# Sums of squares of keys and queries as ScalarE's accumulated output, one token block at a time

## The chip, the core and the metric

The kernel runs on one core of a Trainium2 chip. The core's engines are TensorE (PE; PEld is its weight load), VectorE (DVE), ScalarE (ACT), GpSimd (POOL) and SyncE (SP), which run side by side and wait for each other by semaphores; 16 DMA engines move data. Matmuls write into PSUM, everything else lies in SBUF. The metric is the device time of one execution, in microseconds.

## The reference

Two layers of a diffusion block on 256 context and 256 latent tokens of width 1024. Each layer has a mixer, whose heads read one modulated input, and an MLP of 4096 hidden columns, each behind a residual and a layer norm. Half of the mixer's width are four heads of a gated delta rule of width 128. For those, keys, queries and values go through a convolution over the tokens and a silu; keys and queries are then divided by their norm and rotated (latent tokens only):

```python
def l2norm(x):
    return x * rsqrt(sum(square(x), axis=-1) + 1e-6)

qkv = silu(centred_conv(qkv, conv_w))          # 5 taps over the tokens
q, k, v = split(qkv)                            # (tokens, 4 heads, 128) each
q, k = l2norm(q), l2norm(k)
q, k = rope_2d(q, rope), rope_2d(k, rope)       # latent tokens
q = q * 128 ** -0.5
```

The change lies in the sum of squares of `l2norm`. In the second layer only latent tokens leave the block, so queries are wanted for latent tokens alone.

## The kernel before

The 512 tokens are four blocks of 128 (blocks 0 and 1 context, 2 and 3 latent). Projections are computed with channels on the partitions and tokens in the columns. A float32 product is made of three matmuls (`mm3`, L276 to L278) of operands split in a high and a low part; ScalarE makes the high part of a weight tile (L250), VectorE the low part (L252).

Each layer is a mixer and an MLP. A string in the configuration gives the order in which a mixer's parts are written down (H is a delta-rule head, B and C the gates' two halves, X the end of this stage), but the order in which an engine gets its instructions is laid out by the framework's scheduler, which simulates the engines with its own costs and takes what it thinks is ready. Each engine then runs its list strictly in order. So work of other parts (the projections' matmuls, weight splits, the gates, adaLN matmuls L303) stands between the steps of a head.

`gdn_head(h)` runs a head's key (kind 0), query (kind 1) and value. For key and query the chain of steps is:

- `gdn_conv`: ScalarE copies the projected channels out of PSUM (L530) and scales them by the middle tap (L531); VectorE adds the other four taps (L533); ScalarE takes a tanh (L535), VectorE makes the silu (L536); TensorE transposes four blocks, so that tokens are on the partitions (L540, into PSUM tile `gtr`).
- ScalarE copies `gtr` to SBUF (L550: `ktok` for a key, a rotating buffer shown as `XT` for a query), squares it (L552); VectorE sums each block over its 128 columns (L554) into the four columns of `gss` and adds the epsilon (L555); POOL raises this to the power -0.5 (L231, inside `rsq`), which gives `grs`.
- The rotation of the latent blocks: POOL makes the sine part in two instructions (L561), VectorE the cosine part (L562) and their sum (L563).
- A key is multiplied by `grs` (L565); a query keeps `grs` apart, scaled (`rq`, L567). TensorE transposes the result back (L570, PSUM tile `gtb`), and ScalarE copies it out (L571).

POOL also adds the column mask to the attention bias (L681), 1.85 us in this stage. There are 4 heads x 2 kinds x 2 layers = 16 such places: 12 with four token blocks, 4 (queries of the second layer) with two.

Of the kernel before, what the change touches and what calls it, by code (L numbers as in the profile page):

```python
# [15 lines left out]
AF = mybir.ActivationFunctionType  # L16
ALU = mybir.AluOpType
AX = mybir.AxisListType
# [158 lines left out]
def body(ctx, tc, a, out, dump=None):  # L177
    nc = tc.nc
    V, S, G, PE, SP = nc.vector, nc.scalar, nc.gpsimd, nc.tensor, nc.sync
# [8 lines left out]
    def sm(name):  # L188
        return PP.tile([128, 512], F32, name=name, tag="g", bufs=CFG["g"])
# [37 lines left out]
    def small(shape, name, dt=F32, bufs=3):  # L227
        return P0.tile(shape, dt, name=name, tag="sm_" + name, bufs=bufs)

    def rsq(outp, x, m):  # L230
        G.tensor_tensor(outp, x, m, op=ALU.pow)  # L231
# [237 lines left out]
    def mixer(l, hT, pre, ctx_m):  # L469
# [22 lines left out]
        def ar(name):  # L492
            cnt[0] += 1
            i = cnt[0] % 8
            return XT[:, 4 * i:4 * i + 4].rearrange("p a b -> p (a b)")
# [20 lines left out]
        def gdn_conv(h, kind):  # L516
            b = 3 * h + kind
            lat_only = last and kind == 1
            t0 = 256 if lat_only else 0
            sg = 1 if lat_only else 0  # L520
            if b in pre:
                ps = pre[b]["ps"]
            else:
                ps = proj_T(getw("w_gdn", l, b), t0, "psg")
            psv = ps.rearrange("p (s c) -> p s c", s=2)
            cnt[1] += 1
            cin = cins[:, cnt[1] % CFG["cin"]]
            ac = ar("cacc")
            av = ac.rearrange("p (s c) -> p s c", s=2)[:, sg:]
            S.activation(cin[:, sg:, 2:258], psv[:, sg:], AF.Copy)  # L530
            S.activation(av, psv[:, sg:], AF.Copy, scale=cw[:, b, 2:3])  # L531
            for kk in (0, 1, 3, 4):
                V.scalar_tensor_tensor(av, cin[:, sg:, kk:kk + 256], cw[:, b, kk:kk + 1], av, op0=ALU.mult, op1=ALU.add)  # L533
            th = ar("cth")
            S.activation(th[:, t0:], ac[:, t0:], AF.Tanh, scale=0.5)  # L535
            V.scalar_tensor_tensor(ac[:, t0:], th[:, t0:], 1.0, ac[:, t0:], op0=ALU.add, op1=ALU.mult)  # L536
            q0 = 2 if lat_only else 0
            pt = sm("gtr").rearrange("p (t c) -> p t c", t=4)
            for t in range(q0, 4):
                PE.transpose(pt[:, t], ac[:, 128 * t:128 * t + 128], ident)  # L540
            return pt, q0
# [4 lines left out]
        def gdn_head(h):  # L546
            for kind in (0, 1):
                pt, q0 = gdn_conv(h, kind)
                x = ktok[h] if kind == 0 else ar("qtok").rearrange("p (t c) -> p t c", t=4)
                S.activation(x[:, q0:], pt[:, q0:], AF.Copy)  # L550
                sq = ar("gsq").rearrange("p (t c) -> p t c", t=4)
                S.activation(sq[:, q0:], pt[:, q0:], AF.Square)  # L552
                ss, rs = small([128, 4], "gss", bufs=4), small([128, 4], "grs", bufs=4)
                V.tensor_reduce(ss[:, q0:], sq[:, q0:], axis=AX.X, op=ALU.add)  # L554
                V.tensor_scalar(ss[:, q0:], ss[:, q0:], 4 * NORM_EPS, None, op0=ALU.add)  # L555
                rsq(rs[:, q0:], ss[:, q0:], mh[:, q0:4])
                x_ = x[:, 2:4]
                ra = ar("rope")[:, :256].rearrange("p (t c) -> p t c", t=2)
                hv = lambda ap, i: ap.rearrange("p t (a s c) -> p (t a) s c", a=2, s=2)[:, :, i]
                for i in range(2):  # L560
                    G.tensor_tensor(hv(ra, i), hv(x_, 1 - i), hv(sinT, i), op=ALU.mult)  # L561
                V.tensor_tensor(x_, x_, cosT, op=ALU.mult)  # L562
                V.tensor_tensor(x_, x_, ra, op=ALU.add)  # L563
                if kind == 0:
                    V.tensor_tensor(x, x, rs.unsqueeze(2).to_broadcast([128, 4, 128]), op=ALU.mult)  # L565
                else:
                    V.tensor_scalar(rq[:, q0:, h], rs[:, q0:], 128.0 ** -0.5, None, op0=ALU.mult)  # L567
                pb = sm("gtb").rearrange("p (t c) -> p t c", t=4)
                for t in range(q0, 4):
                    PE.transpose(pb[:, t], x[:, t], ident)  # L570
                S.activation(kqT[h][:, kind].rearrange("p (t c) -> p t c", t=4)[:, q0:], pb[:, q0:], AF.Copy)  # L571
            pt, _ = gdn_conv(h, 2)
            S.activation(vtok[h], pt, AF.Copy, scale=0.5)
# [197 lines left out]
        def run_order(o):  # L771
            for c in o:
                if c in "fBC":
                    {"f": fill, "B": gates1, "C": gates2}[c]()
                    continue
                i = cnt2[c]
                cnt2[c] += 1
                if c == "H":
                    gdn_head(i)
                elif c == "N":  # L780
                    proj_nv(i)
                elif c in "KQ":
                    proj_qk(i, "KQ".index(c))
                elif c == "Z":
                    proj_z(i)
                else:
                    tt = [t for t in CFG["tord"] if t in to]
                    attend(i // len(tt), tt[i % len(tt)], biases[i // len(tt)])
# [576 lines left out]
```

## Time and profile before

| | |
|---|---|
| three runs | 1256.89, 1257.86, 1259.34 us; median 1257.86 |
| profiled execution | 1260.03 us, its span 1258.2 us |
| mean granted TensorE clock | 0.989 |
| delta-rule heads of layer 0 / layer 1 | about 50 to 128 us / 790 to 862 us |

The profile is of one execution. Its page gives busy times by engine; the views used below are the busy time in stretches of the span (windows), the waits of one engine by what it waited for, groups of instructions of one shape, and the timeline. In a timeline row stand the start, the length, the engine, the line, the operation with output and inputs, how many instructions the row holds, and in brackets how long the engine had been idle and what ended that. Lengths overlap on a pipelined engine, so a matmul of 0.39 us may be followed by the next one after 0.23.

### The profile page before, as it was taken

Reading aid. Unit: us, or ns where it says so; the run is one execution under the profiler, and the core shown is the slowest. Engines: PE = TensorE matmul, PEld = TensorE weight load, DVE = VectorE, ACT = ScalarE, POOL = GpSimd, SP = SyncE. Lnnn points to the kernel's source line nnn. Section 1 sums busy time; section 2 is a strip of 40 time slices with the busy share of each in tenths; the row PEclk is TensorE's granted clock in tenths of the full one; section 3 lists DMA queues with packets and bytes.
Section 4 is the critical chain, followed back from the end, with each engine's and each line's share of the span. In section 5 each row is a group of like instructions: output and inputs, shape, how many; then the busy total and the mean of one; then the engine's idle time right before and its main releaser. Section 6 shows DMA issues by size and latency. Waiting matters only on the chain. (4 is left out here: it accounts for less than half of the span.)

```text
span 1258.2 us, 20332 instructions
## 1 busy us (share of the span) xinstructions
PE 1208.7 (96%) x7848; PEld 981.4 (78%) x7848; DVE 865.1 (69%) x1732; ACT 608.7 (48%) x1115; POOL 88.2 (7%) x98
## 2 busy tenths in 40 slices
PE   7999999999999999999999999899999998999997
PEld 3676568887878987787788888676679886898996
DVE  3798697666489954444444478996876768766677
ACT  2465637665446632322322356566466554544551
POOL 0132000100101000000000000222000110000000
PEclk9999999999999999999999999899999998999999
DMA  9623570225166633544533256225730457555552
GB/s 327 233 67 114 171 249 19 64 61 175 64 234 198 220 118 117 157 132 121 158 128 104 97 184 202 84 84 177 268 106 30 138 166 279 179 189 185 189 189 92
DMA packets 62721, 190.91 MB, mean 152 GB/s; under 512 B 7809, under 2 KB 17825, under 8 KB 62625
## 3 DMA queue, kind: packets, MB, share of 16 engines
q1 hardware_dynamic: 62624, 189.62, 45.9%
q8 instruction: 62, 1.02, 0.3%
q14 instruction: 35, 0.28, 0.1%
HBM read 187.46 MB, written 2.13 MB: 151 GB/s over the span
## 5 line engine op out<-in xcount | busy, mean ns | idle before, releaser
L252 DVE TENSOR_TENSOR wlo<-wraw,whi 128x1024 fp32r<-128x1024 f32 x224 | 275.5, 1232 | 185.7 <-ACT whi L250 185.2
L250 ACT ACTIVATE whi<-wraw 128x1024 fp32r<-128x1024 f32 x224 | 236.9, 1059 | 320.1 <-PE pst L278 169.6
L276 PE MATMUL pm<-hhi,whi 128*128 128x256 f32 (+1 forms) x544 | 176.3, 324 | 0.8 <-ACT whi L250 0.7
L278 PE MATMUL pm<-hhi,wlo 128*128 128x256 f32 (+1 forms) x544 | 174.5, 321 | 0.0
L277 PE MATMUL pm<-hlo,whi 128*128 128x256 f32 (+1 forms) x544 | 174.4, 321 | 0.0
L276 PE MATMUL pst<-whi,ah 128*128 128x512 f32 x384 | 150.0, 391 | 0.0
L277 PE MATMUL pst<-wlo,ah 128*128 128x512 f32 x384 | 149.5, 389 | 0.0
L278 PE MATMUL pst<-whi,al 128*128 128x512 f32 x384 | 149.1, 389 | 0.0
L276 PEld LDWEIGHTS pm<-hhi,whi 128*128 128x128 f32 x544 | 103.5, 190 | 14.4 <-issue 5.8
L278 PEld LDWEIGHTS pm<-hhi,wlo 128*128 128x128 f32 x544 | 103.6, 190 | 7.8
L277 PEld LDWEIGHTS pm<-hlo,whi 128*128 128x128 f32 x544 | 103.6, 190 | 7.2
L276 PEld LDWEIGHTS pst<-whi,ah 128*128 128x128 f32 x384 | 72.1, 188 | 15.5 <-issue 0.8
L278 PEld LDWEIGHTS pst<-whi,al 128*128 128x128 f32 x384 | 72.1, 188 | 15.2
L276 PE MATMUL psg<-hhi,whi 128*128 128x512 f32 (+1 forms) x216 | 79.5, 369 | 4.6 <-ACT XT L531 2.3
L277 PEld LDWEIGHTS pst<-wlo,ah 128*128 128x128 f32 x384 | 72.1, 188 | 14.4
L278 PE MATMUL psg<-hhi,wlo 128*128 128x512 f32 (+1 forms) x216 | 79.0, 366 | 0.6 <-DVE wlo L252 0.6
L277 PE MATMUL psg<-hlo,whi 128*128 128x512 f32 (+1 forms) x216 | 79.1, 367 | 0.0
L533 DVE SCALAR_TENSOR_TENSOR XT<-U,cw,XT 128x512 f32<-128x512 f32 (+1 forms) x96 | 65.5, 702 | 1.9 <-ACT XT L531 1.6
L1243 ACT ACTIVATE ah<-mr 128x256 fp32r<-128x256 f32 (+1 forms) x68 | 33.4, 491 | 65.7 <-DVE mr L1241 65.7
L303 PE MATMUL adaps<-wraw,scT 128*32 128x256 f32 x640 | 55.5, 389 | 3.2 <-DMA wraw<-w_ada 3.1
L231 POOL TENSOR_TENSOR rs<-ve,mh 128x1 f32<-128x1 f32 x12 | 12.2, 1018 | 630.4 <-DVE bmv L396 362.5
L1244 DVE TENSOR_TENSOR al<-mr,ah 128x256 fp32r<-128x256 f32 (+1 forms) x68 | 35.1, 516 | 24.3 <-ACT ah L1243 24.1
(672 smaller groups left out, 2387.2 us busy)
## 6 DMA issues: line engine op xcount, KB each, us to landing
wraw<-w SPq DMA_DIRECT2D x140, 512.0 KB
wraw<-w_ada SPq DMA_DIRECT2D x80, 512.0 KB
wraw<-w_gdn SPq DMA_DIRECT2D x27, 512.0 KB
wraw<-w_out SPq DMA_DIRECT2D x24, 512.0 KB
xa<-w_ada SPq DMA_DIRECT2D x32, 256.0 KB
wraw<-w_vz SPq DMA_DIRECT2D x16, 512.0 KB
wraw<-w_na SPq DMA_DIRECT2D x16, 512.0 KB
lnrow<-lnr SPq DMA_DIRECT2D x8, 512.0 KB
```

Of the source, the lines that this page charges most:

```text
L231: G.tensor_tensor(outp, x, m, op=ALU.pow)
L250: S.activation(hi, r, AF.Copy)
L252: V.tensor_tensor(lo, r, hi.bitcast(F32), op=ALU.subtract)
L276: PE.matmul(o, l[0], r[0], start=start, stop=False)
L277: PE.matmul(o, l[0], r[1], start=False, stop=False)
L278: last_mm[:] = [PE.matmul(o, l[1], r[0], start=False, stop=stop).ins]
L303: PE.matmul(st["ps"][32 * g:32 * g + 32, :256], scT[:, k, :], w[:, 256 * g:256 * g + 256], start=(k == 0), stop=(k == 7), tile_position=(0 ...
L533: V.scalar_tensor_tensor(av, cin[:, sg:, kk:kk + 256], cw[:, b, kk:kk + 1], av, op0=ALU.mult, op1=ALU.add)
L1243: S.activation(ah, r, AF.Copy)
L1244: V.tensor_tensor(al, r, ah.bitcast(F32), op=ALU.subtract)
```

## The change

The Square of the whole tile and the reduce on VectorE go. Instead, ScalarE squares each token block by itself, with an accumulated output that writes the sum over the block's 128 columns into one column of `gss`. So at a place with four blocks ScalarE runs four instructions of 128 columns instead of one of 512, and VectorE one instruction less. The buffers stay the same.

```diff
                 S.activation(x[:, q0:], pt[:, q0:], AF.Copy)
                 sq = ar("gsq").rearrange("p (t c) -> p t c", t=4)
-                S.activation(sq[:, q0:], pt[:, q0:], AF.Square)
                 ss, rs = small([128, 4], "gss", bufs=4), small([128, 4], "grs", bufs=4)
-                V.tensor_reduce(ss[:, q0:], sq[:, q0:], axis=AX.X, op=ALU.add)
+                for t in range(q0, 4):
+                    S.activation(sq[:, t], pt[:, t], AF.Square, accum_out=ss[:, t:t + 1])
                 V.tensor_scalar(ss[:, q0:], ss[:, q0:], 4 * NORM_EPS, None, op0=ALU.add)
                 rsq(rs[:, q0:], ss[:, q0:], mh[:, q0:4])
```

The framework lays the instructions out anew. POOL's order in the first head stays as it was; the other engines' lists differ in both mixers. Three places of layer 0 are shown.

VectorE at the first key head (`ktok_456`), in the list before, from the weight split L252 to the key's product with `grs`:

```order
L252 TENSOR_TENSOR wlo<-wraw,whi 128x1024
L554 TENSOR_REDUCE gss<-XT 128x4
L562 TENSOR_TENSOR ktok_456<-ktok_456,cst 128x256
L555 TENSOR_SCALAR gss<-gss 128x4
L536 SCALAR_TENSOR_TENSOR XT<-XT 128x512
L563 TENSOR_TENSOR ktok_456<-ktok_456,XT 128x256
L533 SCALAR_TENSOR_TENSOR XT<-U,cw,XT 128x512
L565 TENSOR_TENSOR ktok_456<-ktok_456,grs 128x512
```

The same stretch of VectorE's list now, with the two rows that follow:

```order
L252 TENSOR_TENSOR wlo<-wraw,whi 128x1024
L562 TENSOR_TENSOR ktok_456<-ktok_456,cst 128x256
L555 TENSOR_SCALAR gss<-gss 128x4
L563 TENSOR_TENSOR ktok_456<-ktok_456,XT 128x256
L565 TENSOR_TENSOR ktok_456<-ktok_456,grs 128x512
L536 SCALAR_TENSOR_TENSOR XT<-XT 128x512
L533 SCALAR_TENSOR_TENSOR XT<-U,cw,XT 128x512 x3
```

The reduce is gone, and the silu product of the query (L536) and a convolution step (L533), which stood ahead of L565, now stand behind it.

TensorE at the same place, one piece of the difference, around the transposes back of the first key (`gtb<-cst,ktok_456`) and those of the first query (`gtr`):

```order
-L276 MATMUL psg<-hhi,whi 128x512
-L277 MATMUL psg<-hlo,whi 128x512
-L278 MATMUL psg<-hhi,wlo 128x512
-L276 MATMUL psg<-hhi,whi 128x512
 L570 MATMUL gtb<-cst,ktok_456 128x128 x4
+L278 MATMUL psg<-hhi,wlo 128x512
 L540 MATMUL gtr<-cst,XT 128x128 x4
```

These and four more rows of the same kind ahead of them stood in front of L570 and now stand behind it: between the key's L540 and L570 there are 13 matmuls, where there were 21. At the third key head there are 14, where there were 22.

VectorE at the third query head, in the list before; the `spt` rows (L617, L618) belong to the gates:

```order
L554 TENSOR_REDUCE gss<-XT 128x4
L618 TENSOR_SCALAR spt<-spt 128x64
L562 TENSOR_TENSOR XT<-XT,cst 128x256
L617 TENSOR_TENSOR spt<-spt 128x64
L555 TENSOR_SCALAR gss<-gss 128x4
L563 TENSOR_TENSOR XT<-XT 128x256
L618 TENSOR_SCALAR spt<-spt 128x64
L567 TENSOR_SCALAR rq<-grs 128x4
```

The same place now:

```order
L555 TENSOR_SCALAR gss<-gss 128x4
L562 TENSOR_TENSOR XT<-XT,cst 128x256
L618 TENSOR_SCALAR spt<-spt 128x64
L567 TENSOR_SCALAR rq<-grs 128x4
L563 TENSOR_TENSOR XT<-XT 128x256
```

L567, which reads POOL's `grs`, has moved ahead of L563, whose result the transposes L570 of blocks 2 and 3 read.

## Rows read from the trace of the kernel before

**Rows 1.** The page, part 1: busy us, share of the span, instructions, by engine.
```profile
PE 1208.7 (96%) x7848; PEld 981.4 (78%) x7848; DVE 865.1 (69%) x1732; ACT 608.7 (48%) x1115; POOL 88.2 (7%) x98
```

**Rows 2.** Windows: length, busy PE, PEld, DVE, ACT, POOL, granted clock, DMA share, GB/s.
```profile
50.00:128.00 78.00, 73.65 (x387) 56.49 (x385) 70.49 (x146) 45.03 (x79) 25.34 (x26) 0.98 0.32 105
128.00:260.00 132.00, 128.15 (x1203) 97.96 (x1202) 97.31 (x250) 81.79 (x205) 6.57 (x8) 1.00 0.37 119
...
790.00:862.00 72.00, 65.32 (x379) 51.82 (x378) 63.99 (x143) 40.63 (x77) 18.84 (x25) 0.95 0.31 99
```

**Rows 3.** TensorE's waits, 40 to 260 us: total, times, longest.
```profile
PE gtb L570 <- DVE ktok L565: 3.2, 2, 1.9
```

**Rows 4.** Timeline, first key head: start, length, engine, line, idle before.
```profile
57.30 1.85 POOL L681 TENSOR_TENSOR bias<-bias,cst 128x768 f32<-128x768 f32 x1
57.38 2.05 DVE L562 TENSOR_TENSOR ktok<-ktok,cst 128x256 f32<-128x256 f32 x1 [0.18 <-POOL XT L561]
...
59.27 0.39 PE L278 MATMUL psg<-hhi,wlo 128*128 128x512 f32 x1
...
59.35 0.16 DVE L555 TENSOR_SCALAR gss<-gss 128x4 f32<-128x4 f32 x1
...
59.50 0.39 PE L276 MATMUL psg<-hhi,whi 128*128 128x512 f32 x1
59.59 1.41 POOL L231 TENSOR_TENSOR grs<-gss,mh 128x4 f32<-128x4 f32 x1 [0.44 <-DVE gss L555]
...
61.03 0.69 DVE L565 TENSOR_TENSOR ktok<-ktok,grs 128x512 f32<-128x512 f32 x1
...
61.78 0.66 PE L570 MATMUL gtb<-cst,ktok 128*128 128x128 f32 x4 [1.89 <-DVE ktok L565]
```

**Rows 5.** Groups by shape, ScalarE and VectorE, 50 to 130 us: busy, mean ns, idle.
```profile
L552 ACT ACTIVATE XT<-gtr 128x512 f32<-128x512 f32 x8 | 4.8, 600 | 0.0
...
L624 ACT ACTIVATE nA<-ad 128x8 f32<-128x8 f32 x2 | 0.4, 196 | 0.0
...
L554 DVE TENSOR_REDUCE gss<-XT 128x4 f32<-128x512 f32 x8 | 5.4, 673 | 0.1
L562 DVE TENSOR_TENSOR ktok<-ktok,cst 128x256 f32<-128x256 f32 x4 | 3.3, 830 | 0.9 <-POOL XT L561 0.9
```

**Rows 6.** Timeline, ScalarE at 130 us.
```profile
130.26 2.17 ACT L806 ACTIVATE dec<-gcr,gcb 128x128 f32<-128x128 f32 x8 [0.80 <-PE gcr L802]
```

**Rows 7.** Timeline, third key and third query.
```profile
93.69 0.68 DVE L565 TENSOR_TENSOR ktok<-ktok,grs 128x512 f32<-128x512 f32 x1
...
94.83 0.60 PE L570 MATMUL gtb<-cst,ktok 128*128 128x128 f32 x4
...
102.03 0.41 DVE L563 TENSOR_TENSOR XT<-XT 128x256 f32<-128x256 f32 x1
...
102.58 0.38 PE L570 MATMUL gtb<-cst,XT 128*128 128x128 f32 x2
...
103.44 0.17 DVE L567 TENSOR_SCALAR rq<-grs 128x4 f32<-128x4 f32 x1 [0.90 <-POOL grs L231]
```

**Rows 8.** Timeline, fourth key.
```profile
112.11 0.68 DVE L554 TENSOR_REDUCE gss<-XT 128x4 f32<-128x512 f32 x1
...
113.04 0.16 DVE L555 TENSOR_SCALAR gss<-gss 128x4 f32<-128x4 f32 x1
...
115.50 0.66 PE L570 MATMUL gtb<-cst,ktok 128*128 128x128 f32 x4 [1.31 <-DVE ktok L565]
```

**Rows 9.** Timeline, first key of layer 1.
```profile
799.69 0.69 DVE L565 TENSOR_TENSOR ktok<-ktok,grs 128x512 f32<-128x512 f32 x1 [0.78 <-POOL grs L231]
...
800.53 0.63 PE L570 MATMUL gtb<-cst,ktok 128*128 128x128 f32 x4 [1.35 <-DVE spt L614]
```

**Rows 10.** Windows behind the first wait, columns as in rows 2.
```profile
62.00:68.00 6.00, 6.00 (x26) 4.82 (x25) 5.26 (x12) 4.21 (x7) 2.91 (x3) 0.72 0.00 0
64.00:66.00 2.00, 2.00 (x7) 1.56 (x6) 1.83 (x5) 2.00 (x4) 1.38 (x3) 0.50 0.00 0
```

## The prediction

> **What bounds the kernel now.** I read the page's busy shares first. TensorE is busy for 96% of the span, VectorE for 69%, ScalarE for 48% [rows 1]. Over the whole program, then, TensorE is the bound, and VectorE time that is taken away is worth nothing by itself.
>
> Next the busy time by stage. The code that is changed runs in two stretches, 50 to 128 us (layer 0) and 790 to 862 us (layer 1). There VectorE is busy for 70.49 of 78 us and 63.99 of 72, while TensorE is idle for 78 - 73.65 = 4.35 us and for 72 - 65.32 = 6.68 us [rows 2]. These two sums are nearly all that a shorter VectorE chain could win. After the first stretch TensorE has another 132 - 128.15 = 3.85 us idle, up to 260 us.
>
> Third, TensorE's waits between 40 and 260 us: the largest is for the transposes of normalised keys (L570), which wait for L565: 3.2 us in 2 waits, the longest 1.9 [rows 3]. So the chain from the Square to L565 does end last at two of the eight places of layer 0.
>
> Then the timeline of the first of these places [rows 4], which the reader should follow by its ends. L562 starts at 57.38, having waited for POOL's L561 and not for the reduce L554, and runs for 2.05 us, to 59.43; beside it POOL adds the bias, L681, from 57.30 to 59.15. Only then comes the epsilon, L555, then POOL's power L231 to 61.00, then L565 to 61.72, then the transposes at 61.78. TensorE had waited for 1.89 us. The reduce isn't what holds this chain: L562 and the busy POOL are.
>
> **What is removed and added.** In 50 to 128 us eight reduces go, at 0.673 us each 5.4 us of VectorE [rows 5]; all 16 places together (12 with four blocks, 4 with two, counted at half) 12 x 0.673 + 4 x 0.34 = 9.4 us. On ScalarE a Square of 512 columns, 0.600 us [rows 5], becomes four of 128 columns. The nearest row is L806, eight 128-column instructions back to back in 2.17 us, 0.27 each [rows 6]: four cost 1.08, which is +0.48 a place, 3.8 us for eight. The trace has no ScalarE instruction with an accumulated output. As a lower bound I take four no dearer than the one now (+0); as an upper one 0.27 plus 0.196 each for writing the sum, the price of a tiny ScalarE row [rows 5]: 1.87, or +1.27. I take +0.48, since L806 has the same shape. ScalarE is busy for 45 of 78 us [rows 2], so this mostly lies in idle time; without that cover it delays the evacuations queued behind it (L530, L531), and with them the VectorE convolutions. From Square to epsilon the chain changes by +0.48 - 0.68 = -0.2 us; the bounds are -0.68 and +0.59.
>
> The Trainium skill, page "ScalarE: Activation LUTs", section "What ACT_TABLE_LOAD costs", gives 186 ns plus 0.833 ns a column, less 93 ns where instructions follow back to back. By that four would take about 0.89 us (an estimate from that page) where L806's row gives 1.08; each chain would be 0.2 us shorter than I count. The row decides.
>
> **What moves: the larger part.** The scheduler lays out TensorE, VectorE and ScalarE anew in both stretches. Four places carry layer 0:
>
> 1. First key. On VectorE a silu product (L536) and a convolution step (L533) no longer stand ahead of L565. On TensorE 13 matmuls stand between the transposes L540 and L570, where there were 21. The release stays near 61.7, because L562 still starts with the end of L561 and still runs beside the bias add, and the power still waits for POOL to finish it. TensorE gets there 8 matmuls earlier, at a pitch of 59.50 - 59.27 = 0.23 us [rows 4], and waits for 3.7 us instead of 1.89. The 8 matmuls run afterwards: **+1.8**. From below: if L562 started 0.7 us sooner and escaped the bias add, the release would be 1.6 us sooner, and the term +0.2.
>
> L562's 2.05 us is odd: the other three of its shape take (3.3 - 2.05) / 3 = 0.42 us [rows 4, 5]. The Trainium skill, page "SBUF — State Buffer", section "Who interferes with whom", says that a VectorE instruction with two SBUF inputs contends with a GpSimd instruction that reads SBUF, and that a reduce never does. The trace agrees as far as L562 beside L681 shows. By that rule removing the reduce leaves the contention where it is (+1.8 stands); were the long row due to the reduce ahead of it, the term would be +0.2.
>
> 2. Third key: 14 matmuls stand ahead of L570 where there were 22. L565 ended at 93.69 + 0.68 = 94.37 and the transposes ran without a wait at 94.83 [rows 7], a slack of 0.46. Eight matmuls earlier is 8 x 0.227 = 1.8: **+1.35**. VectorE's gain of 0.68 here goes against the filler that it did not do at place 1 (L536 and L533, 1.4 us, less one reduce), so I leave it out; with it the term is +0.7.
>
> 3. Third query: L567, which waits for POOL's power, now stands ahead of L563, which the transposes wait for. Before, L567 started at 103.44 after a wait of 0.90, and the transposes had run at 102.58 [rows 7]. Now L567 ends at 103.61, L563 (0.41) at 104.02, and the transposes run 1.45 later, less the 0.2 by which the chain is shorter: **+1.25**. If the power isn't late, 0.
>
> 4. Fourth key, which waited for 1.31 us. The reduce started at 112.11 and the epsilon at 113.04 [rows 8]; now the epsilon needs no reduce ahead of it on VectorE: **-0.9**. Bounds 0 and -1.3.
>
> The other four places have no wait that ends there; I put them at 0. What TensorE did not do in time goes into its idle time after 128 us [rows 2]; of 3.85 us I give it **-0.5** (0 to -1.5), because most of that idle time is in dependent chains that start later too. Layer 0: 1.8 + 1.35 + 1.25 - 0.9 - 0.5 = +3.0.
>
> Layer 1: at the first key the reduce stands between the Square and the power, L565 waits for it, and the transposes waited for 1.35 us [rows 9]; the order on TensorE keeps 38 matmuls there, so the 0.7 us of the reduce is won: -0.7. At the third and fourth key 5 and 8 matmuls fewer stand ahead of the transposes, between 0 and 1.7 us of new wait; I take +0.7, below the middle. Together 0.
>
> Sum +3.0. On the profiled run's own time, 1260.03 us (its span of 1258.2 and 1.8 around it), that is 1263.0. The median of the three runs is 1257.86, which is 2.17 below it; so 1257.86 + 3.0 = 1260.9.
>
> **Rivals.**
> - VectorE's relief wins. In both stretches VectorE is nearly full, and 9.4 us of work leave it. If TensorE follows VectorE there, and not the order laid out at the four places, half of the 4.35 + 6.68 us of idle time goes, and perhaps the half clock after the 1.89 us wait. The place is the stretches' convolutions (L533), which then start up to 0.68 us sooner a place; it decides as soon as the gain per place is passed on at more than half of the 16 places. Time: 1257.86 - 5 = 1253. For it: the VectorE shares. Against it: only 3.2 us of wait names this chain [rows 3], and TensorE's order was laid out for a chain that is shorter than the trace's.
> - No difference. A matmul that moves behind a wait is not lost; the bound engine makes it up where it was idle. If the 3.85 us after 128 us take all of 3.0, the time is 1257.9. Against it: waits in a dependent chain are idle time already spoken for.
> - The clock makes it dearer. After the 1.89 us wait the granted clock was 0.50 from 64 to 66 us (the 1.2 GHz level) and 0.72 on the mean from 62 to 68: 6 x 0.28 = 1.7 us lost [rows 10]. The mean of the whole stretch, 0.98 of 78 us [rows 2], leaves 1.6 us lost, so the 1.31 us wait at the fourth key took no clock. If the new waits at places 2 and 3 drop it as well: +3.4, and with the upper price of the Squares on the four chains (0.6 each) another +2.4: 1260.9 + 5.8 = 1266.7.
>
> **How the numbers follow.** Forecast (+1 to +6): 0.37. Relief: 0.25. No difference: 0.27. Clock and dear Squares: 0.11. A measurement of this kernel can tell about 0.2%, 2.5 us, from no change. Slower 0.37 + 0.11 = 0.48; same 0.27; faster 0.25. The likeliest case alone gives 1259 to 1264. The range of eight in ten reaches down to the relief, 1253, and up to the clock's case, 1267.
>
> **What would show it.** Right: TensorE's wait before the first L570 near 3.7 us and L565 still near 61; L563 behind L567 at the third query and a wait of about 1.3 us there; the stretch after 128 us starting some 3 us later. Four accumulating Squares taking near 1.1 us, no more than 1.9. Wrong: TensorE idle in either stretch falling by 2 us or more; L562 near 0.42 us at the first key; the power starting before 59; or a shift at 128 us that is gone by 260 us.

## The result: 1.1% slower, more than forecast, and the profile after

| | before | changed |
|---|---|---|
| median of 5 runs | 1259.34 us (1256.89 to 1261.70) | 1273.27 us (1269.94 to 1275.02) |
| profiled execution, span | 1260.03, 1258.2 us | 1269.94, 1268.1 us |

The ratio is 1.0110, interval 1.0095 to 1.0126: some 14 us slower, where +3.0 was forecast and the range ended at 1267. The sign is as forecast, the size is not. The profiled execution of the changed kernel is the fastest of its five, so the two traces show 9.9 of the 14 us.

The busy line of the changed kernel's page, which answers to [rows 1]:

```profile
PE 1205.8 (95%) x7848; PEld 977.6 (77%) x7848; DVE 863.2 (68%) x1716; ACT 616.2 (49%) x1211; POOL 87.7 (7%) x98
```

The two busiest engines have no more to do: TensorE has 2.9 us less, VectorE 1.9 us less (the reduces that went were 9.4); ScalarE, which is busy for half of the span, has 7.5 more. The time is lost in waiting. Windows of the changed kernel, as in [rows 2]:

```profile
50.00:128.00 78.00, 67.27 (x329) 51.50 (x328) 64.72 (x131) 46.47 (x128) 20.61 (x25) 0.98 0.28 90
128.00:260.00 132.00, 125.49 (x1205) 96.27 (x1205) 97.68 (x241) 79.79 (x200) 9.66 (x8) 1.00 0.37 123
790.00:862.00 72.00, 61.98 (x380) 52.55 (x379) 63.73 (x134) 44.41 (x113) 17.41 (x22) 1.00 0.32 103
```

TensorE does 67.27 us of work in 50 to 128 us where it did 73.65; VectorE 64.72 where it did 70.49. TensorE's idle time grows from 4.35 to 10.73 us there, and from 3.85 to 6.51 us between 128 and 260 us: 9.0 us together. Where the delay stands is read from two landmarks: the gates' matmul L642, which ends the head stage of each layer, and the first MLP matmul of layer 0 (`pm`). Instances of one line, with shortest, median and longest in ns and the first and last start; before, then changed:

```profile
L642 PE MATMUL pc<-cst,gg x8: 272/273/324, 124.8 to 860.9; 128*64 128x128 f32 x8
```

```profile
L642 PE MATMUL pc<-cst,gg x8: 272/273/323, 130.7 to 867.5; 128*64 128x128 f32 x8
```

```profile
L276 PE MATMUL pm<-hhi,whi x544: 277/283/499, 393.2 to 1227.5; 128*128 128x256 f32 x118, 128*128 128x512 f32 x64
```

```profile
L276 PE MATMUL pm<-hhi,whi x544: 277/283/499, 402.1 to 1237.4; 128*128 128x256 f32 x118, 128*128 128x512 f32 x64
```

Layer 0's head stage ends 130.7 - 124.8 = 5.9 us later; its MLP starts 402.1 - 393.2 = 8.9 us later; layer 1's head stage ends 867.5 - 860.9 = 6.6 us later, the last `pm` is 9.9 late. Layer 0 holds the loss. Up to the end of layer 1's head stage 2.3 us come back in these two traces (the mean clock of its stretch was 0.95 before and is 1.00 now), and behind it they are lost again.

TensorE's waits from 40 to 260 us in the changed kernel (total, times, longest), where [rows 3] showed 3.2 us in 2 waits for the first of them:

```profile
PE gtb L570 <- DVE ktok L565: 6.7, 4, 3.5
PE gtb L570 <- DVE XT L563: 2.4, 3, 1.1
PE gtr L540 <- DVE XT L536: 2.2, 3, 1.0
```

At the first key, rows of the changed kernel that answer to [rows 4]:

```profile
57.36 1.81 POOL L681 TENSOR_TENSOR bias<-bias,cst 128x768 f32<-128x768 f32 x1
57.44 2.02 DVE L562 TENSOR_TENSOR ktok<-ktok,cst 128x256 f32<-128x256 f32 x1 [0.77 <-ACT XT L535]
...
59.38 0.16 DVE L555 TENSOR_SCALAR gss<-gss 128x4 f32<-128x4 f32 x1
...
59.62 1.19 POOL L231 TENSOR_TENSOR grs<-gss,mh 128x4 f32<-128x4 f32 x1 [0.44 <-DVE gss L555]
...
60.85 0.69 DVE L565 TENSOR_TENSOR ktok<-ktok,grs 128x512 f32<-128x512 f32 x1 [0.93 <-POOL grs L231]
...
61.59 1.12 PE L570 MATMUL gtb<-cst,ktok 128*128 128x128 f32 x4 [3.46 <-DVE ktok L565]
```

This is as forecast: L562 takes 2.02 us beside the bias add, the power starts at 59.62 (59.59 before), L565 ends at 61.54 (61.72 before), and TensorE waits for 3.46 us where 3.7 was predicted.

At the second key, where I had put nothing. Before:

```profile
74.28 0.69 DVE L554 TENSOR_REDUCE gss<-XT 128x4 f32<-128x512 f32 x1
...
74.92 0.42 DVE L562 TENSOR_TENSOR ktok<-ktok,cst 128x256 f32<-128x256 f32 x1
...
75.26 0.16 DVE L555 TENSOR_SCALAR gss<-gss 128x4 f32<-128x4 f32 x1
...
75.50 1.44 POOL L231 TENSOR_TENSOR grs<-gss,mh 128x4 f32<-128x4 f32 x1 [0.62 <-DVE gss L555]
...
78.01 0.60 PE L570 MATMUL gtb<-cst,ktok 128*128 128x128 f32 x4
```

Changed:

```profile
77.27 0.25 ACT L554 ACTIVATION_READ_ACCUMULATOR XT<-gtr 128x1 f32 x1
...
77.86 0.42 DVE L562 TENSOR_TENSOR ktok<-ktok,cst 128x256 f32<-128x256 f32 x1 [0.78 <-POOL XT L561]
...
78.21 0.74 DVE L533 SCALAR_TENSOR_TENSOR XT<-U,cw,XT 128x512 f32<-128x512 f32 x1
...
78.87 0.16 DVE L555 TENSOR_SCALAR gss<-gss 128x4 f32<-128x4 f32 x1
...
79.11 1.11 POOL L231 TENSOR_TENSOR grs<-gss,mh 128x4 f32<-128x4 f32 x1 [1.28 <-DVE gss L555]
...
80.25 0.69 DVE L565 TENSOR_TENSOR ktok<-ktok,grs 128x512 f32<-128x512 f32 x1 [0.30 <-POOL grs L231]
...
81.09 0.63 PE L570 MATMUL gtb<-cst,ktok 128*128 128x128 f32 x4 [1.09 <-DVE ktok L565]
```

Two things differ. Before, VectorE used the time in which POOL worked on L561 for the reduce, and L562 followed without a wait; now it sits for 0.78 us at L562, which waits for POOL. And a convolution step (L533, 0.74 us) that stood behind the epsilon L555 now stands ahead of it, although ScalarE's last sum was there at 77.27 + 0.25 = 77.52. The epsilon waits for 1.35 us in the queue with its input ready. So the power starts at 79.11, and TensorE waits for 1.09 us. Which of the two costs this wait is settled below, by the run with the reduce put back in the new lists.

VectorE's own waits from 54 to 124 us say the same for the stage; before, then changed:

```profile
DVE rq L567 <- POOL grs L231: 2.0, 3, 0.9
DVE ktok L562 <- POOL XT L561: 0.9, 2, 0.8
DVE ktok L565 <- POOL grs L231: 0.9, 1, 0.9
DVE wlo L252 <- ACT whi L250: 0.5, 1, 0.5
DVE XT L562 <- POOL XT L561: 0.3, 2, 0.2
```

```profile
DVE rq L567 <- POOL grs L231: 2.6, 3, 0.9
DVE ktok L565 <- POOL grs L231: 2.5, 4, 0.9
DVE XT L562 <- POOL XT L561: 2.3, 2, 1.5
DVE ktok L562 <- POOL XT L561: 1.5, 3, 0.8
DVE wlo L252 <- ACT whi L250: 1.4, 3, 0.7
DVE ktok L562 <- ACT XT L535: 0.8, 1, 0.8
DVE XT L533 <- ACT XT L531: 0.2, 1, 0.2
```

These rows sum to 4.6 us before and 11.3 after: 6.7 us more, mostly for POOL, where 5.4 us of reduces left VectorE [rows 5].

The price of the accumulated Square itself, all 56 of them:

```profile
L554 ACT ACTIVATE XT<-gtr x56: 270/286/315, 55.8 to 862.1; 128x128 f32<-128x128 f32 x56
L554 ACT ACTIVATION_READ_ACCUMULATOR XT<-gtr x56: 203/220/248, 55.9 to 862.3; 128x1 f32 x56
```

Each Square of 0.286 us is followed by an accumulator read of 0.220 us, a second instruction. They overlap: from the first of the second key's four pairs, at 76.37, to the next ScalarE instruction (L535), at 77.36, it is 0.99 us. The forecast was 1.08.

### The profile page after: what moved, and what is told of

Read it like the earlier page. It is cut to its first block, busy times and chain, and to the rows that moved or that the text cites. A ratio compares the mean times of both kernels' runs of the same rounds, so it can differ in the third digit from the quotient of the medians.

```text
span 1268.1 us, 20423 instructions
## 1 busy us (share of the span) xinstructions
PE 1205.8 (95%) x7848; PEld 977.6 (77%) x7848; DVE 863.2 (68%) x1716; ACT 616.2 (49%) x1211; POOL 87.7 (7%) x98
## 4 chain that ended last, share of the span: by engine, by line
PE 71%; DVE 11%; ACT 6%; DMA 3%; POOL 3%; issue 2%; DVEq 0%; SPq 0%; POOLq 0%; ACTq 0%
PE pst L276 7%; PE pst L277 7%; PE pst L278 7%; PE pm L276 7%; PE pm L278 7%; PE pm L277 7%; PE adaps L303 3%; PE pss L717 2%; DVE wlo L252 2%; PE psn L276 1%; PE psn L277 1%; PE psn L278 1%; ACT whi L250 1%; PE pss L697 1%; DVE XT L533 1%
## 5 line engine op out<-in xcount | busy, mean ns | idle before, releaser
L252 DVE TENSOR_TENSOR wlo<-wraw,whi 128x1024 fp32r<-128x1024 f32 x224 | 274.7, 1228 | 190.8 <-ACT whi L250 190.2
L533 DVE SCALAR_TENSOR_TENSOR XT<-U,cw,XT 128x512 f32<-128x512 f32 (+1 forms) x96 | 66.4, 711 | 2.2 <-ACT XT L531 1.8
```

What stands on the lines that cost most here:

```text
L252: V.tensor_tensor(lo, r, hi.bitcast(F32), op=ALU.subtract)
```

## The experiments

To part the edit from the scheduler's new order, each engine's list was held: behind the kernel's body an order-only edge goes from every instruction of TensorE, VectorE, ScalarE and POOL to the next one of a given list. SP's list came out the same by itself. "Old lists" are those of before, "new lists" those of the changed kernel. All ratios are to the kernel before, run on the same chip; differences in us are between medians, some of them from different chips, where the kernel before took 1259.36 to 1259.99 us.

```diff
     with _tile.TileContext(nc) as tc:
         body(tc, a, o)
+        hold_order(tc)    # for each engine: add_manual_dep(next, this, NoSync) along the list
```

**Edit or order.** Accumulated Squares in the old lists: four Squares stand where one stood, the reduce is missing.

> The accumulated Squares, but the lists of TensorE, VectorE, ScalarE and POOL held to those of before (at each place four Squares stand where one stood, and the reduce is simply missing). Theory 'order' (the loss comes from the new lists): 1258 to 1262 us, no different from before, and the first wait before L570 near 1.9 us again. Rival 'price' (the four Squares with their accumulator reads, some 1.0 us of ScalarE instead of 0.5 a place, hold up the chain and the evacuations behind): 1268 to 1274, as the changed kernel.

1262.12 us, 1.0017 (1.0003 to 1.0030): 0.2% slower, at the upper end of the expectation for "order". The first wait is 1.90 us.

The other corner, one Square and the reduce in the new lists:

```diff
+L554 TENSOR_REDUCE gss<-XT 128x4       (ahead of its place's L562 / L555, new VectorE list)
-L554 ACTIVATE XT,gss<-gtr 128x128 x4
+L552 ACTIVATE XT<-gtr 128x512
```

> The other corner: one Square and the reduce on VectorE as before, in the lists of the changed kernel (the reduce put back right ahead of the first of L555 and L562 of its place). Theory 'order': 1270 to 1276 us, as the changed kernel, although no accumulated Square is left. Rival 'price': 1258 to 1263, as before.

1275.57 us, 1.0129 (1.0111 to 1.0147). The lists carry the loss; with or without the accumulated Square each list takes the same time to 0.2%. The second key of this run, new lists with the reduce:

```profile
77.95 0.43 DVE L562 TENSOR_TENSOR ktok<-ktok,cst 128x256 f32<-128x256 f32 x1
...
78.95 0.16 DVE L555 TENSOR_SCALAR gss<-gss 128x4 f32<-128x4 f32 x1
...
79.19 1.11 POOL L231 TENSOR_TENSOR grs<-gss,mh 128x4 f32<-128x4 f32 x1 [1.28 <-DVE gss L555]
...
81.18 0.63 PE L570 MATMUL gtb<-cst,ktok 128*128 128x128 f32 x4 [1.08 <-DVE ktok L565]
```

The reduce is back (at 77.12) and L562 waits for nothing, yet the power starts as late as in the changed kernel and TensorE waits as long. In the old lists with accumulated Squares it is the other way about: L562 waits for POOL for 0.35 us at this place, the epsilon follows right behind it at 75.10, and the transposes run at 77.59 without a wait. So the gap that the missing reduce leaves at L562 does not cost TensorE's wait here; what the new list has and the old has not is the convolution step ahead of the epsilon. It stands there at four of layer 0's eight places (first, second and fourth query, second key), before at none. VectorE's waits from 54 to 124 us are 8.5 us with the old lists and accumulated Squares, 8.1 with the new lists and the reduce: the edit alone brings 3.9 us of waits and the lists alone 3.5, and only with the new lists is time lost.

**Which layer.** The accumulated Squares, lists changed over in the middle of layer 0's MLP, where old and new lists have had the same instructions:

```diff
-list = new
+list = old[:cut] + new[cut:]      # the second of these runs: new[:cut] + old[cut:]
```

> The accumulated Squares with the lists of before up to the middle of layer 0's MLP and those of the changed kernel from there on. By the traces layer 0's mixer is 8.9 us late when its MLP starts, and layer 1 adds little: theory 'order in layer 0' expects 1260 to 1265 us. If the loss of layer 0 is given back later and layer 1 is what counts: 1268 or more.

1261.61 us, 1.0018 (1.0008 to 1.0028): layer 1's new lists cost nothing when layer 0 is old.

> The accumulated Squares with the lists of the changed kernel in layer 0 and those of before in layer 1, the complement of the run with the lists of before in layer 0 (1261.6 us). If the whole loss lies in layer 0's lists: 1271 to 1275 us. If the layers' parts don't add up, for instance because layer 1 gives something back only in its new lists: above 1275.

1268.73 us, 1.0078 (1.0057 to 1.0099), below both expectations. Layer 0's new lists cost 6.6 us by this run (1268.73 - 1262.12) and 11.7 by the other (1273.27 - 1261.61). Layer 0 is the larger part either way; that layer 1's new lists cost 4.5 us only behind a late layer 0 is unexplained.

**TensorE's list.** In the new lists, matmuls pulled ahead of every L570 that waited (65 in all; the expectation says 70):

```diff
+L276..L278 MATMUL psg x8          (pulled up, first key; 2 to 8 at the others)
 L570 MATMUL gtb<-cst,ktok_456 128x128 x4
-L276..L278 MATMUL psg x8
```

> The changed kernel in its own lists, with one edit on TensorE: ahead of each L570 that waited in its trace, 2 to 8 projection matmuls are pulled up from behind it (70 in all over both layers), VectorE's list stays. Were a wait only a matter of where TensorE's matmuls stand, 70 x 0.2 = some 10 us of waiting would be filled and the kernel would take 1262 to 1268 us. If the chain through VectorE is late anyway and the stage ends by it, the waits shrink at these places but come back behind: 1270 to 1275.

1277.21 us, 1.0134 (1.0114 to 1.0154): no better. Its TensorE waits, 40 to 260 us:

```profile
PE gtr L540 <- DVE XT L536: 5.1, 5, 1.3
...
PE gtb L570 <- DVE ktok L565: 1.9, 2, 1.7
```

The waits for L565 fall to 1.9 us, and those for the silu product L536 rise to 5.1. TensorE waits for VectorE one step later, and layer 0's L642 starts at 129.9 us, hardly sooner than in the changed kernel (130.7).

**VectorE's epsilon.** In the new lists, L555 right ahead of its place's L562 (10 places where it wasn't):

```diff
+L555 TENSOR_SCALAR gss<-gss 128x4
 L562 TENSOR_TENSOR ktok<-ktok,cst 128x256
 L533 SCALAR_TENSOR_TENSOR XT<-U,cw,XT 128x512
-L555 TENSOR_SCALAR gss<-gss 128x4
```

> The changed kernel in its own lists, with one edit on VectorE: at every place the epsilon (L555), which needs nothing but ScalarE's sums, stands right ahead of L562 and not behind it and a convolution step. If VectorE's list is the cause (the sums lie ready while L562 waits for POOL and L533 runs, so that POOL's power starts late), the power starts 0.5 to 1.2 us sooner a place, TensorE's waits before L570 shrink and the kernel takes 1264 to 1270 us. If TensorE's list is the cause (matmuls put behind the transposes that wait, and behind the stage), it stays at 1271 to 1275.

1266.71 us, 1.0057 (1.0040 to 1.0075). The second key in this run:

```profile
78.06 0.17 DVE L555 TENSOR_SCALAR gss<-gss 128x4 f32<-128x4 f32 x1 [0.69 <-ACT XT L554]
...
78.31 1.13 POOL L231 TENSOR_TENSOR grs<-gss,mh 128x4 f32<-128x4 f32 x1 [0.19 <-DVE gss L555]
...
80.92 0.63 PE L570 MATMUL gtb<-cst,ktok 128*128 128x128 f32 x4 [0.43 <-DVE ktok L565]
```

The power starts 0.25 us behind the epsilon's start, and TensorE's wait is 0.43 us instead of 1.09. That looked like the cause until the same edit was made in the old lists:

> The accumulated Squares in the lists of before, with the epsilon right ahead of L562 at 14 places; the bias add stays where it was. It separates the two edits of the fastest version. If the earlier epsilon is what makes it fast: 1254 to 1257 us; the first key gains little, since POOL does the bias add ahead of the power. If it is the bias add: 1259 to 1262, as with the epsilon where it was.

1255.27 us, 0.9961 (0.9947 to 0.9975). It is worth 6.8 us in the old lists (1262.12 - 1255.27) and 6.6 in the new (1273.27 - 1266.71). The late epsilon is a fault of both and does not tell them apart. And with the reduce in place, epsilon directly behind it:

```diff
 L554 TENSOR_REDUCE gss<-XT 128x4
+L555 TENSOR_SCALAR gss<-gss 128x4
 L562 TENSOR_TENSOR ktok_456<-ktok_456,cst 128x256
-L555 TENSOR_SCALAR gss<-gss 128x4
```

> The kernel before (one Square, the reduce on VectorE) in its own lists, with the epsilon directly behind the reduce and ahead of L562 at 14 places. If the early epsilon alone is the gain: 1254 to 1257 us, as with the accumulated Squares. If it needs the accumulated Squares, because the reduce still holds the epsilon until POOL has its L561 nearly done: 1258 to 1260.

1253.65 us, 0.9956 (0.9942 to 0.9969), no different from the accumulated one, and faster than both kernels compared here. At its second key the epsilon stands at 74.88, behind the reduce (74.17, 0.67 us):

```profile
75.12 1.11 POOL L231 TENSOR_TENSOR grs<-gss,mh 128x4 f32<-128x4 f32 x1 [0.56 <-DVE gss L555]
```

The power starts at 75.12 where it started at 75.50, and takes 1.11 us instead of 1.44. My rival expectation (the reduce holds the epsilon too long) falls.

**The bias add.** The kernel before with the first L681 behind the power on POOL:

```diff
-L681 TENSOR_TENSOR bias<-bias,cst 128x768
 L231 TENSOR_TENSOR grs<-gss,mh 128x4
+L681 TENSOR_TENSOR bias<-bias,cst 128x768      (in the runs after this one: behind L796)
```

> The kernel before in its own lists, with one edit on POOL: the bias add (L681) stands behind the first key's power instead of ahead of it. If the bias add is what makes L562 take 2.05 us there and holds the power up, L562 takes 0.42 us, the power starts near 58.1, TensorE's wait of 1.89 us falls to 0.5 or less, its clock does not fall to half behind it, and the kernel takes 1255 to 1257.5 us. Rival: the waiting is made up for elsewhere, 1258 to 1260.

1259.88 us, 1.0003 (0.9990 to 1.0015), a miss:

```profile
59.83 1.81 POOL L681 TENSOR_TENSOR bias<-bias,cst 128x768 f32<-128x768 f32 x1
59.90 2.30 DVE L565 TENSOR_TENSOR ktok<-ktok,grs 128x512 f32<-128x512 f32 x1
...
62.25 0.66 PE L570 MATMUL gtb<-cst,ktok 128*128 128x128 f32 x4 [1.86 <-DVE ktok L565]
```

L562 is back at 0.43 us (at 57.88), but now L565 runs beside the bias add and takes 2.30 us instead of 0.69 [rows 4]. The contention went to the next VectorE instruction on the same chain. So the add was put where POOL is idle:

> The kernel before in its own lists, with the first bias add (L681) on POOL put behind the clearing of a buffer (L796) at 125 us, where POOL is idle for 60 us. Put behind the power, it had only moved the contention to L565 (2.30 us there). Now L562 should take 0.42 and L565 0.69 us, the first wait before L570 should be 0.5 us or less and the clock behind it stay at full: 1255 to 1257.5 us. Rival: what is won at 62 us is waited for later in the stage, and the kernel takes 1258 to 1260.

1257.64 us, 0.9985 (0.9971 to 0.9999), just above the expected range. The first wait did fall, to 0.26 us, and the clock from 62 to 68 us was 1.00. With the accumulated Squares:

> The accumulated Squares in the lists of before, with the first bias add at 125 us and the epsilon where it was. If the two edits add up, this takes about 2 us less than the same lists with the bias add at its old place: 1259 to 1261 us. If the bias add alone makes the fastest version: 1254 to 1257.

1258.83 us, 0.9991 (0.9979 to 1.0004), 3.3 us below the same lists without it, where 2 was expected. Both edits together:

> The accumulated Squares in the lists of before, with the epsilon right ahead of L562 at 14 places and the first bias add at 125 us as in the run beside it. If VectorE's missing reduces are worth something once nothing is laid out worse, this is the fastest: 1252 to 1257 us. If TensorE's list, which is that of before, bounds the stages, it is no better than the run beside it: 1255 to 1260.

1254.59 us, 0.9959 (0.9944 to 0.9974): no better than the epsilon alone, though the first key now runs almost through (L562 takes 0.42 us, the transposes wait for 0.19) and TensorE is busy for nearly all of the stage:

```profile
50.00:128.00 78.00, 77.64 (x421) 57.74 (x420) 70.14 (x146) 51.62 (x145) 24.65 (x26) 1.00 0.37 118
```

**What is left between the lists.** The new lists with epsilon early, bias add late, and L567 behind L563 at the four queries where it stood ahead:

> The lists of the changed kernel with three edits: the epsilon ahead of L562, L567 behind L563 at the four queries where it stood ahead, and the first bias add at 125 us. VectorE's late epsilon was worth 6.5 us of the loss; 7 remain. If those are L567's place and the bias add: 1258 to 1262 us. If they are the matmuls that stand behind the stage and the conv steps that now stand ahead of the reduces' old place, it takes 1262 to 1266.

1262.65 us, 1.0022 (1.0010 to 1.0034); 8 us remain to the old lists with the first two edits. TensorE's list mended on top, 25 matmuls pulled:

> The lists of the changed kernel with the epsilon early, L567 behind L563 and the bias add late (1262.65 us), and now 25 matmuls of layer 0 on TensorE pulled ahead of the transposes that still waited in that run's trace, 6 of them at the last one from the work that stood behind the stage. If TensorE's list is most of what is left, now that VectorE's chain is short: 1256 to 1260 us. If pulling only moves the waits on to the next transposes L540, as it did in the unmended lists: 1262 or more.

1262.12 us, 1.0016 (1.0005 to 1.0027), nothing won: TensorE now waits for the silu product (L540 for L536) for 3.0 us in 5 waits. Its transposes L540 of the third query and value stand at 96.50 and 103.77 us, without the 25 matmuls at 96.63 and 103.89: they keep VectorE's rhythm, whatever TensorE has been given to do. The other way about, the forecast's two groups of 8 matmuls put behind the transposes of the fast kernel:

```diff
-L276..L278 MATMUL psg x8          (first and third key, old TensorE list)
 L570 MATMUL gtb<-cst,ktok 128x128 x4
+L276..L278 MATMUL psg x8
```

> The fastest accumulating version (lists of before, epsilon early, bias add late: 1254.6 us, first wait 0.19 us, none at the third key), with one edit on TensorE: the 8 matmuls ahead of L570 at the first and at the third key of layer 0 stand behind it, as in the changed kernel. By the prediction's reckoning the two waits grow by 1.8 us each less the slack, and nothing gives it back: 1256.5 to 1258.5 us. If TensorE makes it up in idle time later: 1254 to 1255.5. If the half clock follows the first wait: 1259 or more.

1258.55 us, 0.9991 (0.9980 to 1.0002), 4.0 us more than without the edit, at the upper end of the expectation. The two transposes wait for 2.0 and 1.1 us. By the end of layer 0's head stage 2.2 us of the loss are there (L642 at 122.0, without the edit at 119.8); where the rest comes from was not followed.

No run has one engine's list from before beside another's from the changed kernel, and none edits ScalarE's list. The engines' shares in the loss are parted only as far as these single edits go.

## Why the prediction was wrong

- **The four places that carry layer 0.** Right in sum, and at three of the four singly. First key: 3.46 us of wait, forecast 3.7. Third key: 1.19, forecast 1.35. Third query: 1.11, forecast 1.25. Fourth key: 0.94, forecast 1.31 - 0.9 = 0.41, so 0.37 was won there and not 0.9. The growth is 1.57 + 1.19 + 1.11 - 0.37 = 3.5 us, the forecast's sum ahead of the give-back 3.5. The run with two groups of matmuls pushed back agrees with this kind of price: 2.0 + 1.1 us of wait where 1.8 + 1.35 was reckoned, 2.2 us by the end of the stage, 4.0 in the whole. None of the signs named for "wrong" came.
- **"The other four places have no wait that ends there; I put them at 0."** This step failed. The second key waits for 1.09 us, the second query for 0.69, the fourth for 0.62, and the value transposes (L540) for 2.2 where they waited for 1.1: 3.5 us more, as much as the four places together. I had read from the trace of before which waits ended there and had not followed VectorE's new list at these places. At the second key and the second and fourth query a convolution step that did not stand between L562 and the epsilon now does, so that POOL's power starts late, and less work is left behind the epsilon to cover it. The missing reduce is not the reason: with the reduce back in these lists the second key's wait is 1.08 us and the whole kernel no faster (1275.57).
- **"VectorE's gain of 0.68 here goes against the filler"**, and **-0.2 us for the chain from Square to epsilon.** The instructions were priced right (0.99 us for four, forecast 1.08), the chain was not: at the second key, copy to epsilon took 75.26 - 73.16 = 2.10 us and now takes 78.87 - 75.89 = 2.98, +0.9 instead of -0.2. In the old lists the same Squares make it 75.10 - 72.66 = 2.44, and in the new lists the reduce makes it 78.95 - 76.00 = 2.95. What sets the epsilon here is its place in VectorE's queue, not the durations of what feeds it.
- **"-0.5" for work made up after 128 us.** Wrong in sign, the second step that failed. TensorE's idle time from 128 to 260 us did not shrink but grew by 2.7 us, and with the 6.4 us ahead of it that makes 9.0 us, as much as the delay of 8.9 us at the MLP. Between L642 and the MLP the delay grows by 3.0 to 8.2 us in all seven traces with new lists in layer 0, in the nine other edited ones by 0.3 at most. Why is open. In the changed kernel's trace some 27 matmuls that ran ahead of layer 0's L642 run behind it (22 of adaLN, 4 value transposes, 1 of a projection), but this was not tried by itself, and the run that pulled six of them forward still has 4.9 us of growth.
- **Layer 1 at 0.** Right where layer 0 has the old lists (1261.61 against 1262.12). Where it has the new ones, which is the case that was forecast, layer 1's new lists cost 4.5 us by the medians (1273.27 - 1268.73), unexplained.
- **Contention.** Right: the bias add beside a VectorE instruction with two SBUF inputs makes that 2.0 to 2.3 us, and the Trainium skill's rule (page "SBUF — State Buffer", section "Who interferes with whom") holds for L562 and for L565 beside it; removing the reduce changed nothing there. Beside POOL's power, which reads four columns, no such price shows: at the first key before, L563 with two SBUF inputs took its usual 0.41 us there.
- **The rivals.** Relief of VectorE did not come: 5.4 us of work went and 6.7 us of waiting came. TensorE did not make the moved matmuls up either: its idle time grew by 9.0 us up to 260 us. The half clock was not the cause: the windows behind the longer wait have 0.79, before 0.72 [rows 10].

What is shown: the new lists cost 11 us with accumulated Squares (1273.27 - 1262.12) and 16 with the reduce (1275.57 - 1259.54); the edit moves either list by 0.2% (2.6 us up in the old, 2.3 down in the new). Pulling TensorE's matmuls up mends nothing, which points to VectorE's queue as what paces the stage in the new lists; a run with VectorE's list alone exchanged is missing. What stays open: 8 us between old and new lists with the epsilon, L567 and the bias add mended. 3.2 of them are the growth behind L642 in that run's trace (none with the old lists); the rest was not taken apart. Why the scheduler put L533 ahead of the epsilon was not tried either.

## What to carry to other kernels

Where a scheduler lays out the program, price an edit in the old order and the new order separately, and hold the lists to measure each: here the edit moved the time by 0.2% either way and the reordering cost 11 to 16 us. On a queue that runs strictly in order, look first at what stands ahead of the short instruction that another engine waits for: the epsilon, moved at 14 places ahead of an instruction that waits for POOL, won 0.4% with the reduce and 0.6% with the accumulated Squares. Work taken from an engine that then waits for the same partner is not won: in the old lists 5.4 us of reduces went, 3.9 us of waits came, and the time did not fall.

## What the runs showed that was not expected

- The clock does not follow from the length of a wait alone. With the old lists and accumulated Squares the first wait was 1.90 us, as before (1.89), yet the window from 62 to 68 us had the full clock, where before it had 0.72 [rows 10]; after 3.46 us of wait it had 0.79. The windows of the old lists with accumulated Squares, then of the changed kernel:

```profile
62.00:68.00 6.00, 5.88 (x32) 4.52 (x31) 4.66 (x11) 5.25 (x15) 2.92 (x3) 1.00 0.00 0
```

```profile
62.00:68.00 6.00, 6.00 (x28) 4.88 (x27) 3.62 (x8) 3.82 (x13) 2.00 (x3) 0.79 0.00 0
```

- Moving a contending instruction by one place on POOL moved the 1.6 us of contention from L562 to L565 whole.
- On ScalarE the accumulated output is a second instruction of 0.20 to 0.25 us, but at the second key a pair follows the other after 0.25 us (0.99 / 4), less than the 0.27 of L806's rows without such an output [rows 6].
